# RWKV inverse: loading the triangles' blocks to four groups of 32 partitions by four transfers instead of one repeated

## The chip, the cores and the metric

One core of a Trainium2 chip runs the whole program. The metric is device time in microseconds of one execution. Before the change three runs took 3285.87, 3290.09 and 3291.71 us, a median of 3290.09.

TensorE (PE) does the matmuls, VectorE (DVE), ScalarE (ACT) and GpSimd (POOL) the rest; each works through its own instructions in order and waits for others by semaphores. SyncE (SP) has the queue on which nearly all DMAs of this kernel are issued, in order as well. The DMAs themselves are carried by 16 DMA engines.

## The reference

One layer of a diffusion transformer block: a feed-forward, a mixer of two linear-attention branches (a retention and an RWKV-7 recurrence, each in both directions), an output projection, and a second feed-forward. 1024 latent tokens and 256 context tokens, width 1024. The change lies in the RWKV branch, whose recurrence is, for each of 2 directions and 8 heads of 64:

```python
def step(s, inp):
    rt, wt, kt, vt, at, bt = inp
    sa = jnp.einsum('zbhvk,zbhk->zbhv', s, at)
    s_new = s * wt[..., None, :] + sa[..., :, None] * bt[..., None, :] + vt[..., :, None] * kt[..., None, :]
    y = jnp.where(is_fwd, jnp.einsum('zbhvk,zbhk->zbhv', s_new, rt), jnp.einsum('zbhvk,zbhk->zbhv', s, rt))
    return s_new, y
...
state, ys = lax.scan(step, state0, xs)
```

## The kernel before

The kernel doesn't step token by token. It takes 64 tokens at a time (a chunk), writes the dependence of a chunk's tokens on each other as a triangular 64x64 matrix per head, inverts that, and has matmuls for the rest. A unit is 128 tokens of one direction, two chunks (`e` is 0 or 1) and 8 heads. There are 10 units for each direction, 20 in all, and `recurrences` goes through them: `ready(i)` calls `prep` (loads, decays, the matrices `g`) and then `inverse`; `join` and `chain` use the inverted blocks, and `readout` finishes a unit's output. `chain` carries the state from unit to unit.

`inverse` treats the two 32x32 diagonal blocks (`f`) of each 64x64 triangle. 2 blocks by 2 chunks by 8 heads are 32 small triangles, and they are laid out so that one partition holds a whole triangle of 32x32 numbers:

- L969, four DMAs on SP: the blocks go from `g` to a scratch in DRAM, `d0` (named `scr` in the profile), 32 KB each, so that they can be read in another layout.
- L970, one DMA on SP: from `d0` to the tile `n` (`invn`), 128 partitions of 4 KB. The 32 triangles are read four times, once for each group of 32 partitions, by a source whose outermost dimension has 4 steps of length zero. Group `j` later treats every fourth row of each triangle.
- L972, four copies on ScalarE, one for each group: the group's rows of `n` to `x` (`invx`).
- L976 and L977, 30 pairs of VectorE steps: the substitution, on all 128 partitions at once.
- L980 and L981, for each group: ones on the diagonal, and a DMA of the result to a second scratch, `d1` (also `scr`).
- L983, four DMAs: the inverted blocks back into `g`.

`join` (L995 to L1002) then adds the off-diagonal 32x32 blocks by small matmuls.

Between the units' work the same engines do the fill, `fill`: the projections of the retention branch and of the gates (`qkvg` and `gates`), big matmuls (L207 to L209, `fps`) whose weights come by DMA (L194, `wraw`), are cast and split by ScalarE (L196, `whi`) and GpSimd (L197, `wlo`), and whose results ScalarE evicts (L782, L785, L803, `gs`).

The order on each engine isn't the order of the code: the framework schedules the program by a timeline of its own before it is compiled, and interleaves units and fill. After that the order is fixed, and each engine waits at an instruction until what it needs has come. An edit to one DMA can so move instructions on all engines.

Of the kernel before, what the change touches and what calls it, by code (L numbers as in the profile page):

```python
# [841 lines left out]
def ab(c):  # L842

    return 0 if c % 2 else 64
# [6 lines left out]
class Rwkv(Mixer):  # L851
# [106 lines left out]
    def inverse(self, g, eng, tmp):  # L958


        nc = self.nc
        d0, d1 = (self.scr.tile([2, 2, 8, 32, 32], F32, tag="scr%d" % i, name="scr%d" % i) for i in range(2))
        n = tmp.tile([P, 32, 32], F32, tag="invn", name="invn", bufs=2)
        x = tmp.tile([P, 8, 32], F32, tag="invx", name="invx", bufs=2)
        t = tmp.tile([P, 72], F32, tag="invt", name="invt", bufs=2)
        ef = [(e, f, slice(ab(e) + 32 * f, ab(e) + 32 * f + 32)) for e in range(2) for f in range(2)]
        blk = lambda e, r: g[r, e, :, :, r].rearrange("i a b t -> i (a b) t")
        for e, f, r in ef:
            nc.sync.dma_start(out=d0[f, e].rearrange("q i t -> i q t"), in_=blk(e, r))  # L969
        nc.sync.dma_start(out=n, in_=d0.rearrange("f e q i t -> (f e q) (i t)").unsqueeze(0).to_broadcast([4, 32, 1024]))  # L970
        for j in range(4):
            nc.scalar.activation(x[32 * j:32 * j + 32], n[32 * j:32 * j + 32, j::4], AF.Copy)  # L972
        for i in range(1, 31):
            w, m = 31 - i, (i + 3) // 4
            tv = t[:, :m * w].rearrange("q (r c) -> q r c", c=w)
            eng.tensor_tensor(out=tv, in0=x[:, :m, i:i + 1].to_broadcast([P, m, w]), in1=n[:, i:i + 1, i + 1:].to_broadcast([P, m, w]), op=ALU.mult)  # L976
            eng.tensor_tensor(out=x[:, :m, i + 1:], in0=x[:, :m, i + 1:], in1=tv, op=ALU.add)  # L977
        for j in range(4):
            r = slice(32 * j, 32 * j + 32)
            eng.memset(x[r].rearrange("q k t -> q (k t)")[:, j::36], 1.0)  # L980
            nc.sync.dma_start(out=d1[:, :, :, j::4].rearrange("f e q k t -> (f e q) k t"), in_=x[r])  # L981
        for e, f, r in ef:
            nc.sync.dma_start(out=blk(e, r), in_=d1[f, e].rearrange("q i t -> i q t"))  # L983
# [565 lines left out]
```

## Time and profile before

| | |
|---|---|
| Median of three runs | 3290.09 us |
| Profiled execution: its own time | 3270.48 us |
| Profiled execution: span | 3268.7 us |
| First and last issue of the load L970 | 1302.6 and 2183.4 us |
| Mean granted clock of TensorE, whole span | 0.937 |
| Mean granted clock of TensorE, 1290 to 2240 us | 0.85 |
| DMA moved in the whole span | 416.57 MB |

The profiled execution is one execution, and its rows add up to its own span. Times in the views are microseconds from the start of the span. In the chain of work, a row gives the start, the length and what it was; for a DMA the length goes from issue to landing. In the view of waits, a row gives who waited for whom, the sum, the number of waits and the longest. In the timeline, a bracket at a row's end gives how long the engine was idle before it and what ended that. Line numbers are those of the kernel before; after the change everything below L970 is one line further down.

### The profile page before, as it was taken

The numbers are of one execution on the slowest core, as the hardware profiler recorded it, in microseconds if no ns is written. First come the engines' busy times: TensorE is split into PE (matmuls) and PEld (weight loads), VectorE is DVE, ScalarE is ACT, GpSimd is POOL, SyncE is SP. The second block draws the span as 40 slices with busy tenths as digits, with TensorE's granted clock in tenths as the row PEclk, the third lists the DMA queues.
The fourth block names the chain that finished last, engine by engine and source line by source line (L and its number), as shares of the span: only waits on it lengthen the run. The fifth ranks groups of instructions, "written<-read, shape, count | busy, mean of one in ns | idle before, by whom it ended". The sixth has DMA issues, their size and how long they took to land.

```text
span 3268.7 us, 47408 instructions
## 1 busy us (share of the span) xinstructions
PE 3037.0 (93%) x17879; PEld 2525.8 (77%) x17879; DVE 2006.5 (61%) x3826; ACT 1050.2 (32%) x1790; POOL 950.0 (29%) x768
## 2 busy tenths in 40 slices
PE   8999999999999998788889888888899899999998
PEld 4888888888887786677667677777787688888877
DVE  4876666444448874788666766755766776675012
ACT  5211111111115474334333333333423533333221
POOL 2111111111113313333332322332223533333442
PEclk9999999999999998888888888798899899999999
DMA  5432222111116246556444444534545244448651
GB/s 207 135 94 91 90 91 81 40 39 39 33 39 233 92 174 202 131 154 173 120 121 110 120 131 110 166 92 124 160 152 163 84 140 146 132 136 288 229 174 61
DMA packets 504557, 416.57 MB, mean 127 GB/s; under 512 B 92264, under 2 KB 401448, under 8 KB 504328
## 3 DMA queue, kind: packets, MB, share of 16 engines
q1 hardware_dynamic: 487776, 401.65, 40.5%
q10 hardware_dynamic: 16552, 11.90, 1.2%
q8 instruction: 141, 2.31, 0.3%
q14 instruction: 88, 0.72, 0.1%
HBM read 309.89 MB, written 99.35 MB: 125 GB/s over the span
## 4 chain that ended last, share of the span: by engine, by line
PE 66%; DVE 15%; DMA 11%; issue 3%; ACT 2%; SPq 2%; POOL 1%; DVEq 0%; ACTq 0%; POOLq 0%
PE psd L207 5%; PE psd L208 5%; PE psd L209 5%; DMA invn<-scr 5%; PE p L208 4%; PE p L209 4%; PE p L207 4%; PE psg L209 3%; DVE invt L976 3%; PE psu L208 3%; PE psg L208 3%; PE psu L209 3%; PE psu L207 3%; PE psg L207 3%; DVE invx L977 2%
## 5 line engine op out<-in xcount | busy, mean ns | idle before, releaser
L197 POOL TENSOR_TENSOR wlo<-wraw,whi 128x512 fp32r<-128x512 f32 (+1 forms) x246 | 437.8, 1790 | 1333.0 <-ACT whi L196 1251.5
L389 DVE SCALAR_TENSOR_TENSOR h<-psd,g,h 128x512 f32<-128x512 f32 (+1 forms) x504 | 313.6, 657 | 273.0 <-PE psd L209 272.8
L196 ACT ACTIVATE whi<-wraw 128x512 fp32r<-128x512 f32 (+1 forms) x246 | 193.8, 804 | 369.3 <-DMA wraw<-in_w_in_dram 88.7
L207 PE MATMUL fps<-uh,whi 128*128 128x512 f32 (+1 forms) x576 | 247.3, 430 | 23.9 <-ACT whi L196 15.0
L207 PE MATMUL p<-v,fac 128*128 128x512 f32 x616 | 242.0, 393 | 11.2 <-ACT v L42 6.1
L209 PE MATMUL fps<-uh,wlo 128*128 128x512 f32 (+1 forms) x576 | 245.5, 427 | 3.3 <-POOL wlo L197 3.3
L208 PE MATMUL p<-v,fac 128*128 128x512 f32 x616 | 242.0, 393 | 4.6 <-DVE v L43 4.6
L208 PE MATMUL fps<-ul,whi 128*128 128x512 f32 (+1 forms) x576 | 243.5, 423 | 0.1
L976 DVE TENSOR_TENSOR invt<-invx,invn 128x60 f32<-128x60 f32 (+5 forms) x600 | 202.5, 340 | 66.1 <-issue 31.0
L209 PE MATMUL p<-v,fac 128*128 128x512 f32 x616 | 241.4, 392 | 0.0
L977 DVE TENSOR_TENSOR invx<-invx,invt 128x60 f32<-128x60 f32 (+5 forms) x600 | 193.6, 325 | 26.3 <-DMA rsw<-gs 6.0
L207 PE MATMUL psd<-hh,whi 128*128 128x512 f32 (+1 forms) x528 | 189.8, 360 | 7.0 <-DVE h L389 6.9
L207 PE MATMUL psg<-uh,whi 128*128 128x512 f32 (+1 forms) x528 | 188.8, 358 | 0.9 <-ACT whi L196 0.9
L208 PE MATMUL psg<-ul,whi 128*128 128x512 f32 (+1 forms) x528 | 189.1, 358 | 0.4 <-POOL ul L259 0.4
L209 PE MATMUL psg<-uh,wlo 128*128 128x512 f32 (+1 forms) x528 | 188.8, 358 | 0.0
L207 PE MATMUL psu<-uh,whi 128*128 128x512 f32 (+1 forms) x528 | 187.7, 356 | 0.2 <-ACT whi L196 0.2
L208 PE MATMUL psu<-ul,whi 128*128 128x512 f32 (+1 forms) x528 | 187.6, 355 | 0.0
L208 PE MATMUL psd<-hl,whi 128*128 128x512 f32 (+1 forms) x528 | 187.1, 354 | 0.0
L209 PE MATMUL psu<-uh,wlo 128*128 128x512 f32 (+1 forms) x528 | 187.1, 354 | 0.0
L209 PE MATMUL psd<-hh,wlo 128*128 128x512 f32 (+1 forms) x528 | 186.8, 354 | 0.0
L207 PEld LDWEIGHTS fps<-uh,whi 128*128 128x128 f32 x576 | 123.5, 214 | 53.0 <-ACT whi L196 17.4
L43 POOL TENSOR_TENSOR fac<-draw,fac 128x512 fp32r<-128x512 f32 x88 | 114.3, 1302 | 138.9 <-ACT fac L42 137.8
(365 smaller groups left out, 7059.6 us busy)
## 6 DMA issues: line engine op xcount, KB each, us to landing
wraw<-in_w_in_dram SPq DMA_DIRECT2D x144, 256.0 KB
modw<-in_w_mod_dram SPq DMA_DIRECT2D x112, 256.0 KB
fraw<-in_ffn_w_gate_dram SPq DMA_DIRECT2D x88, 256.0 KB
hd<-d_hid SPq DMA_DIRECT2D x44, 512.0 KB
draw<-in_ffn_w_down_dram SPq DMA_DIRECT2D x88, 256.0 KB
wraw<-in_ffn_w_gate_dram SPq DMA_DIRECT2D x22, 512.0 KB
wraw<-in_ffn_w_up_dram SPq DMA_DIRECT2D x22, 512.0 KB
wraw<-in_ffn_w_down_dram SPq DMA_DIRECT2D x22, 512.0 KB
```

The lines of the kernel that those rows point to most:

```text
L43: eng.tensor_tensor(out=v[1], in0=x, in1=v[0].bitcast(F32), op=ALU.subtract)
L196: nc.scalar.activation(hi[:, s], raw, AF.Copy)
L197: nc.gpsimd.tensor_tensor(out=lo[:, s], in0=raw, in1=hi[:, s].bitcast(F32), op=ALU.subtract)
L207: mm(ps, w[0][:, ws], x[0][xs], start=start, stop=False)
L208: mm(ps, w[0][:, ws], x[1][xs], start=False, stop=False)
L209: mm(ps, w[1][:, ws], x[0][xs], start=False, stop=stop)
L389: nc.vector.scalar_tensor_tensor(out=hs, in0=ps, scalar=gates()[v][:, m:m + 1], in1=hs, op0=ALU.mult, op1=ALU.add)
L976: eng.tensor_tensor(out=tv, in0=x[:, :m, i:i + 1].to_broadcast([P, m, w]), in1=n[:, i:i + 1, i + 1:].to_broadcast([P, m, w]), op=ALU.mult)
L977: eng.tensor_tensor(out=x[:, :m, i + 1:], in0=x[:, :m, i + 1:], in1=tv, op=ALU.add)
```

## The change

The one load to 128 partitions, repeated by its source, becomes four loads of 128 KB, one to each group of 32 partitions. The same bytes are read and land in the same places.

```diff
         for e, f, r in ef:
             nc.sync.dma_start(out=d0[f, e].rearrange("q i t -> i q t"), in_=blk(e, r))
-        nc.sync.dma_start(out=n, in_=d0.rearrange("f e q i t -> (f e q) (i t)").unsqueeze(0).to_broadcast([4, 32, 1024]))
+        for j in range(4):
+            nc.sync.dma_start(out=n[32 * j:32 * j + 32].rearrange("q i t -> q (i t)"), in_=d0.rearrange("f e q i t -> (f e q) (i t)"))
         for j in range(4):
             nc.scalar.activation(x[32 * j:32 * j + 32], n[32 * j:32 * j + 32, j::4], AF.Copy)
```

The scheduler orders the program anew around it. On SP, at the fourth of the 20 units, the queue before reads as follows (`scr` with a number is the DRAM scratch of one unit, `rsw` and `in_kk` are loads for the fill and for the next unit's `prep`):

```order
L969 DMA scr_11019<-g 32x8x32 x4
L789 DMA rsw<-gs 32x512
L970 DMA invn<-scr_11019 128x1x1024
L790 DMA rsw<-gs 32x512
L789 DMA rsw<-gs 32x512
L878 DMA in_kk<-d_kk 128x4x128
L790 DMA rsw<-gs 32x512
L194 DMA wraw<-in_w_in_dram 128x4x128 x2
L981 DMA scr_10521<-invx 256x1x32 x4
```

And the same place on SP in the changed kernel:

```order
L969 DMA scr_11028<-g 32x8x32 x4
L789 DMA rsw<-gs 32x512
L790 DMA rsw<-gs 32x512
L971 DMA invn<-scr_11028 32x1024
L982 DMA scr_10527<-invx 256x1x32 x4
L971 DMA invn<-scr_11028 32x1024 x2
L984 DMA g<-scr_10527 32x8x32 x4
L971 DMA invn<-scr_11028 32x1024
L878 DMA in_v<-d_v 128x4x128
```

The stores (L982) and the reloads (L984) of the unit before have moved between the four quarters. This is so in three of the 20 units; in a fourth only the store stands between them, and in the other sixteen the four quarters stand in a row.

On ACT, at the second unit, the order before is this (`bt` is an eviction for the same unit, `whi` and `gs` belong to the fill):

```order
L785 ACTIVATE gs<-fps 128x512
L196 ACTIVATE whi<-wraw 128x512
L972 ACTIVATE invx<-invn 32x256 x4
L948 ACTIVATE bt<-btps 128x512 x2
L196 ACTIVATE whi<-wraw 128x512
L782 ACTIVATE gs<-fps 128x512
```

And in the changed kernel:

```order
L785 ACTIVATE gs<-fps 128x512
L196 ACTIVATE whi<-wraw 128x512
L973 ACTIVATE invx<-invn 32x256 x3
L782 ACTIVATE gs<-fps 128x512
L973 ACTIVATE invx<-invn 32x256
L948 ACTIVATE bt<-btps 128x512
L196 ACTIVATE whi<-wraw 128x512
L948 ACTIVATE bt<-btps 128x512
```

The four copies stood together; now an eviction of the fill stands ahead of the last one, and the unit's own evictions are parted by a cast for the fill.

## The prediction

> **What bounds the kernel now.** I read the page first: its span, the busy shares and the chain that ended last.
>
> ```profile
> span 3268.7 us, 47408 instructions
> PE 3037.0 (93%) x17879; PEld 2525.8 (77%) x17879; DVE 2006.5 (61%) x3826; ACT 1050.2 (32%) x1790; POOL 950.0 (29%) x768
> PE 66%; DVE 15%; DMA 11%; issue 3%; ACT 2%; SPq 2%; POOL 1%; DVEq 0%; ACTq 0%; POOLq 0%
> ```
>
> TensorE is busy for 93% of the span, so at first sight nothing but its work counts. But the load that the change touches (invn<-scr) is issued only between 1302 and 2184 us, and a share of the whole span says little about that stage. So I asked for the stage alone, and then for its chain of work and for the waits of ScalarE in it.
>
> ```profile
> 1290.00:2240.00 950.00, 816.92 (x6798) 678.70 (x6798) 664.69 (x1770) 336.97 (x652) 324.13 (x319) 0.85 0.48 130
> by line: DMA invn<-scr 16.0%; DVE invt L976 9.8%; DVE invx L977 8.5%; issue 5.8%; PE fps L207 3.8%; PE fps L209 3.7%; PE fps L208 3.5%; PE gps L923 2.7%; PE q L1020 2.1%; PE q L1018 2.0%; ACT invx L972 2.0%; DMA scr<-g 1.8%; PE u L1025 1.7%
> ACT invx L972 <- DMA invn<-scr: 155.2, 19, 15.2
> ```
>
> The columns of the first row are the window, its length, and the busy time of PE, weight loads, DVE, ACT and POOL, then granted clock, DMA share and GB/s. PE works for 816.9 of 950 us and idles for 133.1. In the same 950 us the chain is led by the load: 16.0% of them, 152 us. ScalarE stands still 155.2 us in 19 waits for it, and it works in order: its evictions and casts for the fill's matmuls stand behind that wait.
>
> ```profile
> 1302.60 12.03 DMA invn<-scr
> 2143.01 11.47 DMA invn<-scr
> 1354.29 1.11 PE L952 MATMUL vtps<-ident,in_v 128*128 128x128 f32 x4 [8.30 <-ACT bt L948]
> 1802.89 1.70 ACT L972 ACTIVATE invx<-invn 32x256 f32<-32x256 f32 x4 [9.08 <-DMA invn<-scr]
> 1805.26 2.07 PE L1018 MATMUL q<-S,ar 128*128 128x128 f32 x8 [8.40 <-ACT y L1039]
> ```
>
> The first two rows are the first and the last of 14 loads on the chain (start, then issue to landing): 152 / 14 = 10.8 us each. The others show how it reaches PE: ACT waits 9.08 us for the load, and PE then sits idle 8.30 or 8.40 us until ACT has done what stood behind it.
>
> To see how much of PE's idle time belongs to the load, I took 20 windows, one for each load, from its issue to 4.3 us later, and 20 more from 4.3 to 15 us after it:
>
> ```profile
> sum 86.00, PE 85.34 PEld 72.38 DVE 55.30 ACT 28.20 POOL 24.31; mean PE 4.27 PEld 3.62 DVE 2.77 ACT 1.41 POOL 1.22
> sum 214.00, PE 126.40 PEld 102.27 DVE 67.73 ACT 79.16 POOL 27.25; mean PE 6.32 PEld 5.11 DVE 3.39 ACT 3.96 POOL 1.36
> ```
>
> In the first 4.3 us PE idles 0.7 us of 86; in the next 10.7 it idles 87.6 of 214. The rest of the stage, 650 us, holds 133.1 - 0.7 - 87.6 = 44.8 us, 6.9%. So two thirds of the idle time stand behind a load that is late, and hardly any in the time in which a quick load would land.
>
> **Why the load is slow.** It moves 512 KB. In this window almost nothing else was in flight:
>
> ```profile
> 2071.00:2073.00 2.00, 2.00 (x11) 1.60 (x10) 1.48 (x5) 0.50 (x1) 0.00 (x0) 1.00 0.25 80
> 2338.26 4.67 DMA rq<-d_q
> 1058.51 1.75 DMA l2r<-in_rwkv_a_dram
> 1621.00 1.97 DMA rsw<-gs
> invn<-scr SPq DMA_DIRECT2D x20, 512.0 KB
> L970 SPq DMA_DIRECT2D invn<-scr x20: 562/576/632, 1302.6 to 2183.4; - x20
> L649 SPq DMA_DIRECT2D l2r<-in_rwkv_a_dram x6: 335/413/420, 1057.1 to 1059.4; - x6
> ```
>
> The share of the 16 DMA engines is 0.25: four of them, as many as the load's outermost dimension, the repeat of 4, has steps. The load of q has the same 128 rows of 4 KB in DRAM and no repeat, and lands in 4.67 us. So the 10.8 us are four engines' work. A transfer to 32 partitions, as each of the new ones is, landed in 1.75 us (from DRAM) and 1.97 us (from SBUF) with rows half as long.
>
> **The change, part by part.**
>
> *Removed*: 20 loads of 10.8 us. *Added*: 80 issues where 20 were. For landing of the last quarter: three issues ahead of it, then its own flight. Low end 3 x 0.41 + 1.75 = 3.0 us; high end 3 x 0.58 + 4.67 = 6.4 us, if the four together fly as long as q's 512 KB. I take 4.3, nearer the low end, for the first three quarters fly while the last is being issued. That saves 10.8 - 4.3 = 6.5 us a load.
>
> What of this reaches the end? By the chain: 14 x 6.5 = 91 us, and two more for what queued behind the four loaded engines:
>
> ```profile
> 1555.79 11.88 DMA in_v<-d_v
> 1933.94 12.38 DMA in_r<-d_r
> 2039.84 3.19 DMA in_v<-d_v
> ```
>
> These two were issued just after a load and took 11.88 and 12.38 us where the same kind takes 3.19; spread over 16 engines the new transfers leave no such backlog: (11.88 - 3.19) + (12.38 - 3.19) = 18 us. Together 109 us by the chain. By PE it is less: if the whole stage idled as its undisturbed part does, 6.9%, it would take 816.9 / 0.931 = 877.4 us, 72.6 less. When the chain is shortened, PE's fill is what is late next, so the smaller number holds: **-72**, 3.6 for each of 20 loads.
>
> *The clock.* After a stall PE runs at half rate for a while:
>
> ```profile
> 1797.00:1805.00 8.00, 0.00 (x0) 0.00 (x0) 0.75 (x7) 2.04 (x5) 0.00 (x0) 0.68 0.63 172
> 1805.00:1813.00 8.00, 7.74 (x33) 6.62 (x34) 7.17 (x22) 4.76 (x9) 5.82 (x6) 0.50 0.30 83
> 1640.00:1653.00 13.00, 12.96 (x90) 11.01 (x89) 7.45 (x17) 3.08 (x6) 5.19 (x4) 0.50 0.50 116
> ```
>
> 8 us without a matmul, then 8 us at clock 0.50, which cost 4 us of work. If every one of the chain's 14 loads costs that, 56 us are to be had; if none does, nothing. The third row speaks for the low end: 13 us at 0.50 with PE busy, and no load near. I take about a third, **-20**. The Trainium skill, page "TensorE: Matmul & The Clock Gate", section "Part 1: The HAM clock gate", says that the throttled state is the default and that activity releases it; by that rule alone the first two rows agree and the whole 56 would come, while the third row doesn't fit it.
>
> *Moved*: the scheduler orders anew. On SP, four of the 20 loads no longer stand together: a store of the inverse before (L982, which waits for VectorE), and in three of them its reload (L984, which waits for the stores' landing) stand between the quarters.
>
> ```profile
> SPq L981 <- DVE invx L980: 72.6, 19, 11.1
> 1357.30 1.92 DMA scr<-invx
> 1372.52 1.86 SPq L969 DMA_DIRECT2D scr<-g x4
> 1300.72 1.79 DMA scr<-g
> ```
>
> A held quarter waits 72.6 / 19 = 3.8 us for VectorE, 4 x 0.58 for the issues, 1.92 for the landing and 1.9 for the reloads' issues (as L969's four, of the same size, in the third row): some 10 us. It costs nothing where VectorE was done before. I let all four lose what was gained: 4 x 3.6 = **+14**. On ACT some of the four copies (L973) are parted by an eviction or a PE-bound copy; since one L972 copy takes a quarter of 1.70 us and the parted one waits for a later quarter anyway, I cost it at nothing, and at 1 us a load, 20 in all, if that cover is gone. The 60 additional issues are 60 x 0.58 = 35 us of SP's time; SP waits far longer than that for others in this stage (72.6 us in the row above alone), so they are hidden; uncovered they cost 35 us. VectorE's 600 + 600 steps of the inverse, the stores and the reloads stay as they are.
>
> *A rule against the change.* The rows of l2r and rsw put a 32-partition transfer at under 2 us. The Trainium skill, page "DMA: Bandwidth & Descriptors", section "Rules for kernel authors", advises one 128-partition transfer instead of several to parts of the partitions, since those share the same engines and serialize. By that rule the sum would be that of the third rival below; by the same section's rule on the outermost dimension, a leading broadcast of 4 keeps a DMA on at most 4 engines, with which the 0.25 agrees, and the sum would be mine.
>
> **Sum**: -72 - 20 + 14 = -78 us. The profiled execution took 3270.5 us (span 3268.7), which gives 3192; the median of the runs shown is 3290.1, 0.6% above it, and the same difference gives **3212 us**.
>
> **Rivals.** *The clock comes back in full*: -72 - 56 + 14 = -114, 3176 us. The rows of 1797 to 1813 speak for it, that of 1640 against.
>
> *The quarters serialize*: each flies after the one before has landed, 4 x 1.97 = 7.9 us, saving 2.9 of 10.8 a load; of 72 us remain 72 x 2.9 / 6.5 = 32, 3258 us. For it: all are issued on one queue. Against it: the four stores ahead of each load are issued within 1.86 us, and the last of them lands 1.79 us after its issue (the two last rows of the fence above), where one by one they would take four times that.
>
> *SP becomes the bound* (the slower side): behind the held quarters on SP stand the loads of the next unit and the fill's weights. The 35 us of issues come onto the path, and four held quarters land at 4.3 + 10 = 14.3 us, 3.5 later than now, +14; the other sixteen loads give only half of 16 x 3.6, 29, as weights come late. 35 + 14 - 29 = +20, 3310 us. It decides from the point where the issues and holds on the path cost more than the loads give back. For it: SP works in order and was waited for. Against it: DMA issues were on 2% of the chain.
>
> *It doesn't do what it says*: the quarters use four engines again, so only the three issues come on top, and nothing is gained: 3290 us. Against it: 1.75 us for 64 KB to 32 partitions, where four engines at the load's rate, 512 KB in some 10 us, would need 1.3 us for the packets alone, which is close enough that I can't exclude it.
>
> **How the numbers follow.** My forecast 0.60 (3180 to 3245), full clock 0.14 (3176), serialized 0.14 (3258), SP 0.08 (3310), no spread 0.04 (3290). The range goes from 3160, the clock's case with its own spread, to 3275, above the serialized case, and leaves out SP and no spread, 0.12, and some tails. A measurement here can tell about 0.2%, 7 us, from no change. Faster by more: 0.60 + 0.14 + 0.14 = 0.88; within: 0.04; slower: 0.08.
>
> **What would show it.** In the profile after: the load on the chain at 3 to 6 us instead of 10 to 12; ACT's wait for it at some 50 us instead of 155; PE's idle time in the stage at about 65 us instead of 133, and the stage 70 to 90 us shorter; no in_v or in_r at 12 us; granted clock in the stage above 0.85, slightly by my sum, clearly by the first rival. What would make it wrong: the last quarter landing later than 7 us, SP's waits growing by tens of us, or new gaps of PE behind other waits in place of these.

## The result and the profile after

The changed kernel takes 3172.41 us (median of four runs, 3164.72 to 3174.22), the kernel before 3287.98 (four runs, 3269.60 to 3291.71): a ratio of 0.9655, 95% interval 0.9615 to 0.9695. That is 115.6 us less. Beside later kernels it was timed again: 3170.99 against 3280.48, ratio 0.9663, 0.9637 to 0.9689.

The profile of the changed kernel, in the views that carried the prediction. First the stage by windows (columns: window, length, busy time of PE, weight loads, DVE, ACT, POOL; clock, DMA share, GB/s), the chain of work in it by line, ACT's wait for the load, and the load's issues:

```profile
1290.00:2140.00 850.00, 775.71 (x6844) 648.20 (x6844) 659.08 (x1787) 339.72 (x651) 318.41 (x313) 0.88 0.51 142
by line: DVE invt L977 9.4%; DVE invx L978 9.0%; issue 5.0%; PE fps L209 4.3%; PE fps L207 4.2%; PE fps L208 4.1%; PE gps L923 2.7%; DVE g L926 2.6%; DMA invn<-scr 2.1%; PE q L1021 2.1%; PE u L1026 2.1%; PE q L1019 1.8%; DVE S L1035 1.7%; D
ACT invx L973 <- DMA invn<-scr: 28.4, 25, 4.9
L971 SPq DMA_DIRECT2D invn<-scr x80: 312/419/1115, 1303.3 to 2054.1; - x80
```

With some 6,800 matmul records, as many as in the 950 us before, the stretch is 850 us long. PE's idle time in it is 850 - 775.7 = 74.3 us, where it was 133.1; its busy time fell too, by 41 us, at a clock of 0.88 instead of 0.85. The load went from 16.0% of the chain to 2.1%, and ScalarE's longest wait for it from 15.2 to 4.9 us.

Two rows of the chain in the changed kernel show single quarters and a load that was once held up behind the old transfer, and two rows by windows show what the DMA engines do while four quarters fly:

```profile
1855.72 2.88 DMA invn<-scr
1598.58 3.50 DMA in_r<-d_r
2026.50:2030.00 3.50, 3.50 (x24) 3.03 (x23) 1.36 (x3) 3.04 (x6) 0.77 (x1) 1.00 1.02 240
1442.80:1446.50 3.70, 3.70 (x42) 3.16 (x42) 2.13 (x7) 1.57 (x3) 1.42 (x3) 0.98 0.92 249
```

A quarter lands 2.8 us after its own issue in the median and 4.4 at most, no load of a unit's inputs takes over 6.3 us any more, and the engines' share is 0.92 to 1.02 where four engines alone had shown 0.25. Other loads and stores fly in these two windows as well, so the share isn't the load's alone. How many engines the load itself runs on is told by the updates of its semaphore, which the trace holds one by one: every load of the kernel before had 4 late ones, as many as the engines that the 0.25 stands for, and every quarter has 16. Measured by the last of them, from the first issue on, the load lands after 5.41 us on average (median 4.7), before 10.95. Of 134 weight loads (wraw) in the stage, 26 took more than 8 us before, and none does now.

The same updates show what those slow loads waited for. With the loads of the units' inputs, 47 took over 8 us before, and 36 of these have exactly 4 of their 16 updates later than that. A weight load issued at 1303.8 us, just behind the first load of the blocks, has 12 updates by 4.8 us after its issue, and the other four at 10.1, 10.7, 11.0 and 11.3. So its parts on twelve engines were quick, and those on four stood behind the repeated load.

The four loads whose quarters stand apart on SP are seen in its timeline (start, length, instruction):

```profile
1412.25 0.45 SPq L971 DMA_DIRECT2D invn<-scr  x1
1412.79 2.55 SPq L982 DMA_DIRECT2D scr<-invx  x4
1415.38 1.06 SPq L971 DMA_DIRECT2D invn<-scr  x2
1416.72 1.79 SPq L984 DMA_DIRECT2D g<-scr  x4
1418.56 0.45 SPq L971 DMA_DIRECT2D invn<-scr  x1
```

The last quarter is issued 6.3 us after the first, and the load lands after 8.8. The other three take 8.5, 9.2 and 6.8 us. In all four SP goes on to the stores within 0.1 us of the quarter ahead of them: it had not to wait for VectorE there.

### The profile page after: what moved, and what is told of

It reads as the page before. It is cut to its first block, busy times and chain, and to the rows that moved or that the text cites. A ratio compares the mean times of both kernels' runs of the same rounds, so it can differ in the third digit from the quotient of the medians.

```text
span 3172.4 us, 47494 instructions
## 1 busy us (share of the span) xinstructions
PE 3002.3 (95%) x17879; PEld 2501.0 (79%) x17879; DVE 1990.7 (63%) x3826; ACT 1055.1 (33%) x1792; POOL 951.5 (30%) x768
## 4 chain that ended last, share of the span: by engine, by line
PE 35%; DVE 11%; DMA 4%; issue 2%; ACT 1%; SPq 1%; POOL 1%; DVEq 0%; ACTq 0%; POOLq 0%
PE p L208 4%; PE p L207 4%; PE p L209 4%; DVE invt L977 3%; PE psd L207 3%; PE psd L209 3%; PE psd L208 3%; DVE invx L978 2%; PE fps L209 1%; PE fps L207 1%; PE fps L208 1%; PE gps L923 1%; PE ops L207 1%; PE ops L208 1%; PE ops L209 1%
## 5 line engine op out<-in xcount | busy, mean ns | idle before, releaser
L207 PE MATMUL fps<-uh,whi 128*128 128x512 f32 (+1 forms) x576 | 239.8, 416 | 8.4 <-ACT whi L196 6.6
L209 PE MATMUL fps<-uh,wlo 128*128 128x512 f32 (+1 forms) x576 | 239.1, 416 | 5.0 <-POOL wlo L197 5.0
L977 DVE TENSOR_TENSOR invt<-invx,invn 128x60 f32<-128x60 f32 (+8 forms) x600 | 196.4, 332 | 38.2 <-ACT invx L973 19.6
L978 DVE TENSOR_TENSOR invx<-invx,invt 128x60 f32<-128x60 f32 (+8 forms) x600 | 189.2, 320 | 15.6 <-DMA invn<-scr 1.2
L376 ACT ACTIVATE hh<-sg 128x512 fp32r<-128x512 f32 (+1 forms) x66 | 36.9, 559 | 364.8 <-DVE sg L374 307.6
```

The source lines that it names most:

```text
L207: mm(ps, w[0][:, ws], x[0][xs], start=start, stop=False)
L209: mm(ps, w[1][:, ws], x[0][xs], start=False, stop=stop)
L376: nc.scalar.activation(hh, s, AF.Copy)
```

## The experiments

Three things changed at once: the number of engines that a load runs on, the number of transfers, and the order that the scheduler made. Each experiment is told with its edit; lines of a diff are against the kernel named ahead of it.

### One transfer on 16 engines, in the old order (e1_one_wide)

Against the kernel before. The dimension of the 32 triangles becomes the outermost of the source, the repeat stands inside it.

```diff
-        nc.sync.dma_start(out=n, in_=d0.rearrange("f e q i t -> (f e q) (i t)").unsqueeze(0).to_broadcast([4, 32, 1024]))
+        nc.sync.dma_start(out=n, in_=d0.rearrange("f e q i t -> (f e q) (i t)").unsqueeze(1).to_broadcast([32, 4, 1024]))
```

> One transfer of 512 KB as before, but the 32 triangles are the source's outermost dimension and the repeat of 4 stands inside it. Partition p then holds triangle p/4 and not p mod 32, so what is inverted differs from the reference. The order of instructions on all five engines is word for word that of before. Theory 1 (spread: the load was slow because it ran on four of the 16 DMA engines): 16 engines finish it, it lands 4 to 5.5 us after its issue, ACT's wait for it falls from 155 to under 50 us, and the kernel takes 3160 to 3195 us. Theory 2 (order: the gain came from what the scheduler did with four transfers): the order is that of before, so 3270 to 3295 us. Theory 3 (the split: four transfers overlap where one can't): the load still takes over 8 us, 3250 to 3295 us.

Measured: 3162.23 us, ratio 0.9634 (0.9605 to 0.9664). The kernel does the work of before in the same steps, but on other rows of the triangles than the inverse needs, so it answers what the time hangs on and can't be used as it is. All 20 loads end with 16 updates, after 4.52 us on average. ScalarE's wait and the stage (to the last matmul of `chain`) of this kernel:

```profile
ACT invx L972 <- DMA invn<-scr: 55.6, 16, 10.5
1290.00:2201.00 911.00, 831.86 (x7329) 696.63 (x7330) 696.94 (x1841) 363.54 (x701) 335.43 (x326) 0.89 0.50 142
```

Theory 1 holds, and it stands alone: with not one instruction in another place on any engine and not one transfer more, the whole gain is there. Neither the new order nor the split was needed for it. ScalarE's wait of 55.6 us is a little above the 50 expected. Whether one wide transfer beats four (3162 against 3171 to 3172 us) these intervals don't tell.

### Four transfers, on four engines each (e2_four_narrow)

Against the changed kernel. A gap of 32 numbers behind each 8 triangles keeps the scratch's 4 groups a dimension of their own.

```diff
-        d0, d1 = (self.scr.tile([2, 2, 8, 32, 32], F32, tag="scr%d" % i, name="scr%d" % i) for i in range(2))
+        d0 = self.scr.tile([4, 8224], F32, tag="scr0", name="scr0")
+        d1 = self.scr.tile([2, 2, 8, 32, 32], F32, tag="scr1", name="scr1")
...
-            nc.sync.dma_start(out=d0[f, e].rearrange("q i t -> i q t"), in_=blk(e, r))
+            nc.sync.dma_start(out=d0[2 * f + e, :8192].rearrange("(q i t) -> i q t", q=8, i=32), in_=blk(e, r))
...
-            nc.sync.dma_start(out=n[32 * j:32 * j + 32].rearrange("q i t -> q (i t)"), in_=d0.rearrange("f e q i t -> (f e q) (i t)"))
+            nc.sync.dma_start(out=n[32 * j:32 * j + 32].rearrange("q i t -> q (i t)"), in_=d0[:, :8192].rearrange("g (q x) -> g q x", q=8))
```

> Four transfers as in the change, but the scratch in DRAM has a gap of 128 bytes after each 8 triangles, so that the source's outermost dimension has 4 steps. Theory 1 (spread): each quarter runs on four engines again, the last one lands 11 to 13 us after the first issue, PE's idle time in the stage is 120 us or more, and the kernel takes 3275 to 3320 us. Theory 2 (order) and theory 3 (split): there are four transfers and nearly the order of the change, so 3165 to 3200 us.

Measured: 3233.47 us, ratio 0.9854 (0.9829 to 0.9880). The quarters end with four updates each, and the load lands after 9.50 us on average, not 11 to 13. The stage to its last `chain` matmul, and ACT's wait:

```profile
1290.00:2254.00 964.00, 839.71 (x7259) 699.11 (x7259) 671.09 (x1830) 362.28 (x696) 337.17 (x326) 0.86 0.48 134
ACT invx L974 <- DMA invn<-scr: 108.6, 61, 8.7
```

Theories 2 and 3 fall as an account of the whole gain: with four transfers on four engines each the kernel is 62 us slower than the change, and ScalarE waits for the load once more. Theory 1 had the direction and not the size, for this kernel is still 48 us faster than the one before. Its load lands 1.45 us earlier than there, and 4 of 135 weight loads took over 8 us, not 26, perhaps since most of its loads are issued over some 2 us and not at once. How much of the 48 us is that and how much the order was not separated. The order is near that of the change, not the same: SP's instructions other than these loads stand 3.3 places on average from where the change has them, and 10.5 in the kernel before.

### Two transfers, on two engines (e3_two_narrow)

Against the kernel before.

```diff
-        nc.sync.dma_start(out=n, in_=d0.rearrange("f e q i t -> (f e q) (i t)").unsqueeze(0).to_broadcast([4, 32, 1024]))
+        for j in range(2):
+            nc.sync.dma_start(out=n[64 * j:64 * j + 64], in_=d0.rearrange("f e q i t -> (f e q) (i t)").unsqueeze(0).to_broadcast([2, 32, 1024]))
```

> Two transfers of 256 KB to 64 partitions each, each repeating its source twice. Theory 1 (spread): each runs on two engines, and if they are the same two, 128 packets of 4 KB by 2 engines at some 0.25 us each land after 16 to 21 us; 14 loads on the chain get 5 to 10 us longer, so 3360 to 3430 us. If the two transfers take different engines, it is as before, 3275 to 3300. Theory 3 (split): two overlap better than one, so between the kernels, 3200 to 3270 us.

Measured: 3373.57 us, ratio 1.0275 (1.0241 to 1.0308), as theory 1 had it where both transfers run on the same two engines. Each ends with two late updates; counted from the first issue, the first lands after 9.7 us on average and the second after 15.3. The chain of its stage by line starts with the load again:

```profile
by line: DMA invn<-scr 23.3%; DVE invt L977 10.0%; DVE invx L978 9.2%; issue 4.5%; PE gps L923 4.3%; PE fps L209 3.2%; PE fps L207 3.0%; PE fps L208 2.9%; DMA scr<-g 2.7%; DMA rsw<-gs 2.5%; PE q L1021 2.3%; DMA in_r<-d_r 2.3%; PE q L1019 2.
```

### The load delayed, on 16 engines (e4_twice)

Against the changed kernel.

```diff
-        for j in range(4):
+        for j in (0, 1, 2, 3, 0, 1, 2, 3):
             nc.sync.dma_start(out=n[32 * j:32 * j + 32].rearrange("q i t -> q (i t)"), in_=d0.rearrange("f e q i t -> (f e q) (i t)"))
```

> The change, with each quarter loaded twice over (the second time the same bytes to the same place). All transfers run on 16 engines, so nothing queues on four of them; only the landing is later: the second pass waits for the first and lands after 8 to 10 us instead of 5.4. Theory A (the delay of the load itself is what counts): about (9 - 5.4) / (10.95 - 5.4) = 0.65 of the gain of 115 us is lost, 3230 to 3260 us. Theory B (the backlog on the four engines, which held up the other loads, is what counts): 3170 to 3195 us, the upper end by 80 more issues on SP.

Measured: 3203.27 us, ratio 0.9759 (0.9730 to 0.9787): between the two theories. The load lands after 8.13 us, 2.7 later than in the change, and the kernel takes 31 to 32 us more, with no weight load over 8 us. If the delay is all that costs here, at some 11.5 us for each us, the 5.5 us of delay in the kernel before are worth about 63 us, and the rest of the 110 came from elsewhere. The 63 is an estimate: this kernel also issues 80 transfers more and is ordered anew (SP's other instructions stand 6.9 places on average from where the change has them), and neither was separated.

### The backlog alone (e5_backlog)

Against the changed kernel.

```diff
         for j in range(4):
             nc.sync.dma_start(out=n[32 * j:32 * j + 32].rearrange("q i t -> q (i t)"), in_=d0.rearrange("f e q i t -> (f e q) (i t)"))
+        junk = self.scr.tile([P, 1024], F32, tag="junk", name="junk")
+        nc.sync.dma_start(out=junk, in_=d0.rearrange("f e q i t -> (f e q) (i t)").unsqueeze(0).to_broadcast([4, 32, 1024]))
```

> The change, and behind the four quarters one more transfer of the kind that was removed (512 KB, source repeated 4 times outermost), from the scratch to another scratch in DRAM that nothing reads. The quarters land as in the change, some 5.4 us; but four engines are loaded for some 10 us more in each unit, and the loads issued behind it have to pass there. Theory A (only the delay of the load itself costs): 3170 to 3185 us, no more than 20 more issues. Theory B (the backlog on the four engines is the rest of the gain: doubling the quarters cost 31 us for 2.7 us of delay, 11 us for each, so 5.5 us of delay explain some 63 of 115 us): 3205 to 3235 us, with weight loads and unit loads of over 8 us as in the kernel before.

Measured: 3229.88 us, ratio 0.9849 (0.9823 to 0.9874), 59 us more than the change beside it (c_after, 3170.99). The load itself still lands after 5.28 us, but 8 of 15 loads of r, 5 of 17 of the decays (m) and 11 of 134 weight loads take over 8 us. ScalarE's waits for the three, which sum to 71.9, 28.4 and 21.9 us in the change, have grown, though the load of the blocks (invn) lands no later:

```profile
ACT whi L196 <- DMA wraw<-in_w_in_dram: 94.5, 33, 8.9
ACT invx L975 <- DMA invn<-scr: 51.5, 24, 7.2
ACT w L891 <- DMA m<-d_td: 45.6, 11, 7.1
```

Theory B holds: only one wait of 2.9 us in the whole stage is put down to the added transfer itself, and it costs over half of the gain, because what is issued behind it also has a part on the four loaded engines. Of 30 loads of weights and unit inputs over 8 us, 22 have exactly 4 updates later than that, as in the kernel before. Delay, an estimated 63, and backlog, 59, make 122 us; the measured gain beside them is 110. The added transfer also writes 512 KB to DRAM in each unit, which the old load did not, so the 59 is rather a high value. The order is close to the change's (SP's other instructions are 1.7 places off on average), but not the same.

> The changed kernel once more, beside the others of this call: 3165 to 3180 us by every theory.

That control is the second timing given above.

### Two attempts to go further (e6_x_by_dma, e7_wide_rows)

The first, against the changed kernel, loads each group's rows by DMA instead of copying them on ScalarE:

```diff
         for j in range(4):
-            nc.scalar.activation(x[32 * j:32 * j + 32], n[32 * j:32 * j + 32, j::4], AF.Copy)
+            nc.sync.dma_start(out=x[32 * j:32 * j + 32], in_=d0[:, :, :, j::4].rearrange("f e q k t -> (f e q) k t"))
```

> The change, with each group's rows of the triangles loaded to their tile by four more transfers (32 KB, 128-byte pieces) from the same scratch, in place of ScalarE's 80 copies. If ScalarE's wait for the load (28 us now) and its copies (33 us) still cost: 3140 to 3165 us. If they are hidden and SP's 80 more issues count: 3175 to 3200 us.

Measured: 3220.96 us, ratio 0.9824 (0.9795 to 0.9854), 50 us slower than the change and beyond both expectations. Taking the copies off ScalarE gained nothing that this order and these issues didn't cost again. Its load lands after 5.80 us, little later, and PE's idle time in the stage is 107 us. VectorE, which begins the inverse, now waits for the new transfers:

```profile
DVE invx L981 <- DMA invx<-scr: 25.0, 10, 6.2
L973 SPq DMA_DIRECT2D invx<-scr x80: 537/607/1587, 1305.8 to 2088.2; - x80
```

80 x 0.607 = 49 us of SP's time is about what was lost, but how much of it, and how much of the new order on all engines, makes the 50 us was not separated.

The second, against the kernel before, takes the wide load of e1_one_wide and fits the rest to it:

```diff
+        nc.sync.dma_start(out=n, in_=d0.rearrange("f e q i t -> (f e q) (i t)").unsqueeze(1).to_broadcast([32, 4, 1024]))
+        rows = lambda d, j: d[:, :, :, j::4].rearrange("f e q k t -> (f e q) k t")
+        for j in range(4):
+            nc.sync.dma_start(out=x[j::4], in_=rows(d0, j))
...
+        eng.tensor_tensor(out=x, in0=x, in1=self.cst["dia"], op=ALU.add)
+        for j in range(4):
+            nc.sync.dma_start(out=rows(d1, j), in_=x[j::4])
```

> One transfer of 512 KB on 16 engines as in e1_one_wide, made right: partition p holds triangle p/4 and treats every fourth row from p mod 4, the group's rows are loaded by four transfers to every fourth partition in place of ScalarE's copies, the diagonal's ones are added from a constant in one step of VectorE, and four transfers store from every fourth partition. By the spread theory the load lands in 4 to 5 us with one issue, ScalarE never waits for it: 3140 to 3165 us, ahead of the change. If transfers of 128-byte pieces to every fourth partition are slower than to 32 in a row, or the mask's step and its wait come onto the path: 3170 to 3200 us.

Measured: 3189.34 us, ratio 0.9718 (0.9695 to 0.9740), 18 us slower than the change and within the second of the two ranges expected; which of the reasons named there it was, or the new order, was not separated. The load lands after 4.32 us, and the units are done earlier, the last `chain` matmul at 2163 us, but the fill is not: its last matmul comes at 2195 us, where the change has both by 2189. Apart from e1_one_wide, whose inverse differs, no kernel here is faster than the change.

### What makes PE run at half rate (e8_filled, e9_filled_after)

The same edit to both kernels: five matmuls of no use ahead of the unit's second transposes, 100 in all.

```diff
             ps = pp.tile([P, 2, 2, P], F32, tag="mm", name="btps")
+            for i in range(5 * h0 // 2):
+                nc.tensor.matmul(ps.rearrange("p a b x -> p (a b x)"), K.ident, bk[:, :2].rearrange("p h c x -> p (h c x)"), start=True, stop=True)
```

> The kernel before, with five more matmuls of 128x512 in each unit, of no use (they write a PSUM tile that the transposes behind them overwrite), shortly ahead of the point where PE often runs dry while ScalarE waits for the load. They give PE up to some 5 us to do in 20 places. Idle theory (PE's half rate comes from the time in which it has nothing to do): idle time in the stage falls from 143 us to 80 to 110, the time at half rate from 305 us to 190 to 260, and the kernel pays little for 100 matmuls, 3270 to 3310 us. Burst theory (half rate comes from what follows the load on the engines, the inverse on VectorE and small matmuls): half rate stays at 290 to 330 us, and the matmuls are paid in full, 3340 to 3390 us.

> The changed kernel with the same 100 matmuls of no use. Its gaps are few (72 us idle in the stage), so they fill little. Idle theory: idle time falls a little, to 50 to 65 us, half rate from 213 us to 160 to 200, and the kernel takes 3210 to 3250 us. Burst theory: half rate stays at 205 to 230 us and the matmuls are paid in full, 3240 to 3290 us.

Measured: 3330.20 us, ratio 1.0163 (1.0142 to 1.0183), for the kernel before with them, 3218.58 us, ratio 0.9820 (0.9801 to 0.9839), for the changed one. The stages to the last `chain` matmul: the kernel before, the same filled, the change, the same filled.

```profile
1290.00:2302.00 1012.00, 868.83 (x7352) 725.59 (x7352) 691.52 (x1845) 363.77 (x705) 333.40 (x327) 0.85 0.47 128
```

```profile
1290.00:2342.00 1052.00, 918.09 (x7434) 731.38 (x7433) 660.09 (x1815) 356.41 (x677) 335.67 (x325) 0.87 0.44 120
```

```profile
1290.00:2189.00 899.00, 823.80 (x7227) 687.90 (x7226) 667.51 (x1806) 353.02 (x674) 334.82 (x325) 0.88 0.50 140
```

```profile
1290.00:2213.00 923.00, 865.88 (x7361) 687.01 (x7360) 654.43 (x1806) 351.23 (x666) 330.17 (x322) 0.92 0.48 135
```

The added matmuls take 94.18 us of PE's time in the changed kernel and lengthen its busy time by only 865.9 - 823.8 = 42: PE's own work took 52 us less, at a clock of 0.92. In the clock records of the trace the time at half rate in the stage falls from 212 to 147 us there, and from 305 to 263 in the kernel before. The 65 us less at half rate are worth at most 65 / 2 = 32 us of work; where the other 20 come from is not shown.

So the half rate is not tied to what follows the load, which is all still there; work of this kind on PE lessens it. The changed kernel came out as the idle theory had it in time and in idle time (923 - 865.9 = 57 us), with still less half rate. The kernel before fits neither theory: it paid 54 us (3330.2 against 3276.2), between the two ranges. Its idle time hardly fell (143 to 134 us), since PE was never idle just ahead of the added matmuls, and its next pause of over 1 us came 1 to 25 us behind them; its half rate fell all the same.

What the half rate goes with is pauses of some length. PE's pauses of 2 us or more in these stages number 28 in the kernel before and 23 in the same filled, 14 in the change and 10 in the same filled. In 28, 22, 13 and 9 of them half rate sets in during the pause or within 4 us of its end. The expectation that gaps cost half rate afterwards stands; what exactly the clock responds to, and why a stretch of half rate lasts anything from 3 to 17 us in the kernel before, stays open.

The stage of each kernel in numbers (landing from the trace's semaphore updates, idle time by the windows above or the like):

| Kernel | Engines per transfer | Load lands after, us | Time, us | PE idle in the stage, us | Clock there |
|---|---|---|---|---|---|
| e1_one_wide | 16 | 4.52 | 3162 | 79 | 0.89 |
| change | 16 | 5.41 | 3171 | 75 | 0.88 |
| e4_twice | 16 | 8.13 | 3203 | 97 | 0.87 |
| e5_backlog | 16, and 4 behind | 5.28 | 3230 | 115 | 0.86 |
| e2_four_narrow | 4 | 9.50 | 3233 | 124 | 0.86 |
| before | 4 | 10.95 | 3280 | 143 | 0.85 |
| e3_two_narrow | 2 | 15.34 | 3374 | 209 | 0.80 |

## Why the prediction was right, and where it was off

**Why the load was slow**: right. Four engines, by the repeat of 4 in the outermost place: e1_one_wide moves the repeat inside and runs on 16, e2_four_narrow brings an outermost 4 back and runs on four again. The rule of the Trainium skill (page "DMA: Bandwidth & Descriptors", section "Rules for kernel authors") that an outermost dimension of few steps, such as a leading repeat, keeps a DMA on at most that many engines agrees with the 4, 2 and 16 semaphore updates. The advice of the same section not to split a transfer over parts of the partitions, since the parts serialize, would by itself have kept the slow load. Here the parts overlap: a quarter lands 2.8 us after its issue in the median, and four that stand together after 4.7 us on average. Against a load that already runs on 16 engines the split brought nothing: one wide transfer lands after 4.52 us, the four quarters after 5.41 over all 20 loads. (The prediction puts that advice down to its third rival; the rival in which the quarters serialize is the second in its list.)

**Landing at 4.3 us**: 5.41 on average; the sixteen loads that stand together took 4.0 to 5.8, 4.7 on average. **The four held loads**: they landed after 6.8 to 9.2 us, not 14.3, since VectorE was done with the inverse before.

**Idle time, -72 and +14 for the held loads**: in the stretches compared, 133.1 to 74.3, -59 against -58. That the sum fits so well is partly luck, for two misses cancel in it. A cost of the held loads doesn't show: e1_one_wide holds none of its loads back and has no less idle time in its stage, 79 us against 75. And the -72 was some 13 us too much, for PE's idle share fell to 74.3 / 850 = 8.7%, not to 6.9%. That the gain came through two ways, the load's own delay and what queued behind it, was underrated: the prediction gave the backlog 18 us by the chain, from two loads, and e5_backlog shows up to 59.

**The clock, -20**: this term was mis-sized. PE's busy time fell by 816.9 - 775.7 = 41 us, and the clock accounts for nearly all of it: the stretch before has 288 us at half rate and the one after 212, and 76 us less are worth 38 us of work. The measured 3172 us lies within the range given, but outside the 3180 to 3245 of the forecast itself. It is next to the 3176 us of the rival in which the clock comes back in full, to which the prediction gave 0.14; that rival's 56 us were too much in their turn. The row held against this rival, 13 us at half rate from 1640 on with PE busy and no load near, was misread. What stands just ahead of it is a pause:

```profile
1632.00:1640.00 8.00, 5.60 (x34) 4.38 (x33) 6.46 (x14) 5.60 (x11) 2.49 (x2) 0.96 0.30 99
1639.01 0.46 PE L1018 MATMUL q<-S,ar 128*128 128x128 f32 x2 [2.40 <-DVE S L1034]
```

PE idles for 2.40 of these 8 us, until 1639.0, and half rate sets in at 1639.4. VectorE ended that pause, not the load, so the row shows half rate that the change need not remove, but none that comes without a pause.

**From one execution to the median, +20**: the profiled execution before took 3270.5 us, and the prediction carried its distance to the median over to the changed kernel. The profiled execution of the change took 3174.2, 1.8 above its median. Between the two profiled executions the gain is 96 us, between the medians 115.6. So of the 40 us between forecast and result, 21 are the clock and about 20 the choice of the execution from which the sum was made.

**The rivals**: serialized quarters fell (a load lands 4.7 us after its first issue where its quarters stand together, not 7.9; its 3258 us were also summed without the clock and the held loads). SP as the bound fell with the time itself. Its wait for VectorE at the stores went from 72.6 to 56.2 us, with 60 issues more; its wait for ScalarE at L804, from 81.2 us in the stage before, grew to 106.4, a sign that the prediction had named, and the kernel is faster all the same. No spread fell with the 16 updates.

```profile
SPq L982 <- DVE invx L981: 56.2, 21, 8.1
SPq L804 <- ACT gs L803: 106.4, 21, 8.6
```

## What to carry to other kernels

Look at how many DMA engines a slow load keeps busy, not only at its bytes: here a share of 0.25 in a quiet window, and an outermost dimension of 4, told that it could be spread, and both reordering the dimensions and splitting did it. Count in the gain also what is issued behind such a load (up to 59 us here), and the clock that comes back when the matmul engine pauses less (38 us). Before a sum is carried from one profiled execution to a median, see whether that execution is a quick one among its kind.

## What was not expected of the hardware

A transfer for which hardly anything waits cost 59 us, by filling four engines on which the loads behind it have a part too. Two transfers on two engines each landed after 15.3 us, less than the 16 to 21 worked out from the packets' times on four. And 94 us of useless matmuls lengthened PE's busy time by 42 us and the kernel by 48; less half rate accounts for at most 32 of the 52 us that PE's other work took less.
